# Reordering a two-layer decoder trunk: the order of all work taken from another model, attention's side work dealt by a planner, head halves joined by transfers and POOL

## The chip, the cores and the metric

The kernel runs on one core of a Trainium2 chip. That core has five engines that run at the same time, each with a queue of its own that it works off strictly in order: TensorE (PE; its weight loads are shown apart as PEld), VectorE (DVE), ScalarE (ACT), GpSimd (POOL), and SyncE (SP), which here only issues DMA transfers. The metric is the time of one execution on the device in microseconds; a profile is one such execution, recorded.

## The reference

The program computes a decoder trunk of two layers for 512 tokens of width 1024, in fp32:

```python
h = x
for i in range(2):
    if i == 0:   # RetNet heads and mLSTM heads, chunkwise, one output projection
        h = h + ab_mixer(rms_norm(h, ab_norm_g), ...)
    else:        # sparse attention: 16 query heads, 2 key groups
        h = h + nsa_mixer(rms_norm(h, nsa_norm_g), ...)
    h = h + conv_ffn(rms_norm(h, ffn_norm_g[i]), ...)       # gated, D_FF 2816
    e = rms_norm(p[i] @ ple_w[i], ple_norm_g[i])            # per-layer embedding
    h = h + sigmoid(rms_norm(h, ple_gate_norm_g[i]) @ ple_w_gate[i]) * e

# inside nsa_mixer, for each head and block of 128 queries
o = g[..., 0:1] * o_cmp + g[..., 1:2] * o_slc + g[..., 2:3] * o_win
```

Of the three branches of attention, o_cmp attends to 31 compressed blocks of keys, o_slc to selected blocks, o_win to a window. With 512 tokens the selection takes all blocks and the window reaches all earlier tokens, so o_slc and o_win are two causal softmax attentions over different keys and values.

## The kernel before, in words

Activations stand transposed in SBUF: tiles of 128 features by 512 tokens. Each fp32 matrix product is three matmuls (`mm3`, L148 to L150): both operands are split in a high part, copied to fp32r by ScalarE (`split`, L129), and a low part, the difference, made by VectorE or POOL (L130); high by high, high by low, low by high add up in one PSUM bank. Weights come by 512 KB transfers on SP into a pool of three and are split in the same way (`load`); `lo_seq` says which engine makes the low part. PSUM is dealt as four banks "a", three "b", one "o".

Attention (`nsa_mixer`) goes in steps. Each of the 16 heads has six units, a unit being a block j of 128 queries with one branch or both (96 units in all). A step does the scores of one unit: two matmuls and one that adds the mask (L933 to L935) into an "a" bank, the negative maximum on VectorE (L936), the exponential on ScalarE (L938). When both branches of a block are done, VectorE takes the reciprocal of the sums (L948) and POOL multiplies the probabilities by it and by the gate (L950). Four steps later (`LAG`) TensorE transposes the probabilities into a "b" bank (L961), and ScalarE and VectorE split them into `pt` tiles (L129, L130). Two steps after that the values matmuls (L983) add up in the "o" bank, with two for the compressed branch (L971, L972). A head's output stands in that bank as two halves of 64 rows that have to be added: ScalarE copies one half (L987), VectorE adds the other (L991); every second head, ScalarE and POOL split the pair into `y` tiles for the output projection.

Other work is placed between these steps by step numbers written out by hand (`START`): the products of the per-layer embedding, the query norm of the second eight heads (sums of squares, factor L842 to L848, multiplication on POOL L854, high part on ScalarE L859, low part on VectorE L860), the transpositions of queries (L867), the compressed branch's scores (L887 to L906, eight heads at a time), and the output projection of the first eight heads. The program order is only where the framework starts: its scheduler fixes, before anything is compiled, the order in each engine's queue, by a model of what is ready when and by priorities (`high_priority`, `behind`).

## Time and profile before

| | |
|---|---|
| median of 3 runs | 1390.86 us (1386.83 to 1391.09) |
| profiled execution | 1388.07 us, span 1385.9 us |
| TensorE busy | 1362.8 us, 98% of the span |
| VectorE, ScalarE, POOL busy | 848.2 (61%), 641.3 (46%), 361.3 us (26%) |
| mean granted clock of TensorE | 0.997 |

The span reaches from the first to the last instruction; the execution's own time holds a little more. A busy share is an average over stages with different limits: the mixer of the first layer up to about 200 us, its MLP and embedding gate to about 640, the second layer's projections and compressed keys to 757, attention from 757 to 954, then the output projection, MLP and gate of the second layer. Rows of the trace give a matmul from its issue to its last result, so rows of one engine overlap. A name before `<-` is what an instruction writes, those behind it what it reads; buffer numbers are left out in the trace and stand in the order as `ps_6885`.

### The profile page before, as it was taken

The page shows a single profiled execution, that of the slowest core. Times are in us where ns is not written, and L with a number is a line of the kernel's source. Part 1 is how long each engine was busy: PE and PEld are TensorE (multiplying, and loading weights), DVE is VectorE, ACT ScalarE, POOL GpSimd, SP SyncE. Part 2 cuts the span into 40 slices and gives each one's busy share as a digit, 9 for nine tenths or more (in the row PEclk, how much of TensorE's full clock was granted, in tenths as well). Part 3 has the DMA queues.
Part 4 walks back from the last instruction along what each step waited for, and adds up shares of the span by engine and source line. Part 5 has one row for each costly group of instructions (what it writes and reads, how often), then busy time and mean ns, then how long its engine had stood idle before and what let it go on. Part 6 is the DMA issues. An engine that isn't in the chain of part 4 may idle for free.

```text
span 1385.9 us, 17930 instructions
## 1 busy us (share of the span) xinstructions
PE 1362.8 (98%) x6702; PEld 1119.7 (81%) x6702; DVE 848.2 (61%) x1354; ACT 641.3 (46%) x1125; POOL 361.3 (26%) x360
## 2 busy tenths in 40 slices
PE   9999999999999999999999899999999999999998
PEld 7878788888888888887878677777888888888887
DVE  6765756566356435567858988676565446534555
ACT  5357426444124323455455787676444223313441
POOL 4356502132031101121111755544122022101120
PEclk9999999999999999999999999999999999999999
DMA  6432233232322332233343100111233223333232
GB/s 217 148 104 93 90 98 111 81 106 92 106 83 100 102 96 88 86 119 118 93 138 120 46 2 32 31 32 31 92 97 101 92 79 119 92 96 99 80 107 76
DMA packets 40031, 127.96 MB, mean 92 GB/s; under 512 B 4740, under 2 KB 5380, under 8 KB 39944
## 3 DMA queue, kind: packets, MB, share of 16 engines
q1 hardware_dynamic: 39656, 126.68, 28.8%
q8 instruction: 53, 0.87, 0.2%
q14 instruction: 34, 0.28, 0.1%
q10 hardware_dynamic: 288, 0.14, 0.0%
HBM read 122.60 MB, written 3.15 MB: 91 GB/s over the span
## 4 chain that ended last, share of the span: by engine, by line
PE 85%; DVE 5%; issue 4%; ACT 3%; POOL 3%; DMA 1%; POOLq 0%; ACTq 0%; DVEq 0%
PE ps L148 26%; PE ps L149 25%; PE ps L150 25%; PE ps L961 2%; PE ps L983 2%; ACT pr L938 1%; PE ps L933 1%; PE ps L934 1%; DVE nmx L936 1%; DVE pt L130 1%; POOL y L130 1%; POOL pr L950 1%; ACT wh L129 1%; POOL acc L196 1%; DVE wl L130 1%
## 5 line engine op out<-in xcount | busy, mean ns | idle before, releaser
L148 PE MATMUL ps<-y,wh 128*128 128x512 f32 (+1 forms) x1112 | 434.3, 391 | 1.5 <-ACT y L206 0.6
L149 PE MATMUL ps<-y,wh 128*128 128x512 f32 (+1 forms) x1112 | 431.5, 388 | 0.6 <-POOL y L130 0.6
L150 PE MATMUL ps<-y,wl 128*128 128x512 f32 (+1 forms) x1112 | 431.0, 388 | 0.0
L129 ACT ACTIVATE wh<-wr 128x1024 fp32r<-128x1024 f32 (+2 forms) x223 | 230.2, 1036 | 411.3 <-PE ps L149 344.8
L130 DVE TENSOR_TENSOR wl<-wr,wh 128x1024 fp32r<-128x1024 f32 (+2 forms) x202 | 247.6, 1228 | 46.3 <-ACT wh L129 45.8
L148 PEld LDWEIGHTS ps<-y,wh 128*128 128x128 f32 x1112 | 208.9, 188 | 45.0 <-ACT wh L129 1.0
L150 PEld LDWEIGHTS ps<-y,wl 128*128 128x128 f32 x1112 | 208.8, 188 | 43.6 <-DVE wl L130 0.2
L149 PEld LDWEIGHTS ps<-y,wh 128*128 128x128 f32 x1112 | 208.9, 188 | 43.0 <-POOL y L130 1.1
L1136 POOL TENSOR_TENSOR sc<-sc,rb 128x512 f32<-128x512 f32 x44 | 56.9, 1293 | 476.2 <-ACT sc L1135 476.2
L148 PE MATMUL ps<-gh,wh 128*128 128x512 f32 x352 | 136.9, 389 | 0.0
L149 PE MATMUL ps<-gl,wh 128*128 128x512 f32 x352 | 136.9, 389 | 0.0
L150 PE MATMUL ps<-gh,wl 128*128 128x512 f32 x352 | 136.9, 389 | 0.0
L196 POOL TENSOR_TENSOR acc<-acc,sc 128x512 f32<-128x512 f32 x48 | 74.5, 1553 | 223.6 <-ACT sc L194 223.0
L1151 DVE TENSOR_TENSOR hp<-hp,ps 128x512 f32<-128x512 f32 x48 | 33.0, 688 | 130.3 <-PE ps L150 130.3
L950 POOL TENSOR_SCALAR pr<-pr,sm,gate 128x512 f32<-128x512 f32 (+3 forms) x128 | 78.3, 622 | 74.3 <-DVE sm L948 53.0
L1137 DVE TENSOR_TENSOR sc<-ps,sc 128x512 f32<-128x512 f32 x44 | 30.4, 692 | 92.2 <-POOL sc L1136 85.2
L1129 DVE TENSOR_TENSOR a<-ps,rb 128x512 f32<-128x512 f32 x44 | 30.4, 690 | 92.3 <-PE ps L150 89.5
L150 PEld LDWEIGHTS ps<-gh,wl 128*128 128x128 f32 x352 | 66.1, 188 | 13.8
L148 PEld LDWEIGHTS ps<-gh,wh 128*128 128x128 f32 x352 | 66.1, 188 | 13.7
L149 PEld LDWEIGHTS ps<-gl,wh 128*128 128x128 f32 x352 | 66.1, 188 | 13.6
L1135 ACT ACTIVATE sc<-sc 128x512 f32<-128x512 f32 x44 | 27.8, 632 | 100.8 <-DVE sc L1134 100.8
L938 ACT ACTIVATE pr<-ps,nmx 128x512 f32<-128x512 f32 (+3 forms) x128 | 67.0, 528 | 13.7 <-DVE nmx L936 7.8
(288 smaller groups left out, 2000.8 us busy)
## 6 DMA issues: line engine op xcount, KB each, us to landing
wr<-in_w_up_dram SPq DMA_DIRECT2D x88, 512.0 KB, 3.6
wr<-in_w_down_dram SPq DMA_DIRECT2D x32, 512.0 KB, 3.5
wr<-in_w_plg_dram SPq DMA_DIRECT2D x16, 512.0 KB, 3.6
wr<-in_w_down_dram SPq DMA_DIRECT2D x16, 384.0 KB, 3.0
hp<-in_xT_dram SPq DMA_DIRECT2D x16, 256.0 KB, 4.0
wr<-in_w_abo_dram SPq DMA_DIRECT2D x8, 512.0 KB, 3.6
wr<-in_w_dram SPq DMA_DIRECT2D x8, 512.0 KB, 3.6
wr<-in_w_q_dram SPq DMA_DIRECT2D x8, 512.0 KB, 4.0
```

The lines of the kernel that those rows point to most:

```text
L129: self.nc.scalar.activation(hi, src, AF.Copy)
L130: (eng or self.nc.vector).tensor_tensor(lo, src, hi.bitcast(F32), ALU.subtract)
L148: mm(out, ah, bh, start=first, stop=False)
L149: mm(out, ah, bl, start=False, stop=False)
L150: mm(out, al, bh, start=False, stop=last)
L196: eng.tensor_tensor(n.acc, n.acc, sq, ALU.add)
L938: nc.scalar.activation(pr[:, b], s[:, b], AF.Exp, bias=nmx[:, b : b + 1], accum_out=sm[:, bs[b] : bs[b] + 1])
L950: nc.gpsimd.tensor_scalar(prs[b], prs[b], sm[:, b : b + 1], gate[:, j, hd, 1 + b : 2 + b], ALU.mult, ALU.mult)
L1129: nc.vector.tensor_tensor(a, pa, n.b, ALU.mult)
L1136: nc.gpsimd.tensor_tensor(c, c, n.b, ALU.mult)
L1137: nc.vector.tensor_tensor(c, pb, c, ALU.mult)
L1151: nc.vector.tensor_tensor(self.h[m], self.h[m], ps, ALU.add)
```

## The change

- The scheduler orders all engines' queues by its timeline model (one argument of `TileContext`).
- The units of a head come in the order of blocks 3, 3, 2, 2, 1, 0 instead of 3, 3, 1, 2, 2, 0, and the values of a pair of blocks are issued as the branches of a unit come due. For the blocks 0 and 1 one ScalarE and one VectorE instruction split both branches.
- In place of the step numbers a planner in the kernel deals the side work: for every step it keeps what TensorE, VectorE, ScalarE and POOL (T, V, S, G) have to do in ns, and puts a job at the first step where the backlog over `PACE` per step stays within `SLACK`.
- The compressed branch goes in four groups of four heads.
- A head's whole 128 x 512 output is copied by ScalarE; three transfers per pair of heads on SP bring the halves to the rows where they are added; POOL adds, casts and subtracts. The last pair is joined on VectorE and ScalarE.
- Seven weights in attention get their low part from POOL (`load_late`), four before. The query norm's eight low parts of the second half go from VectorE to POOL, and so do the eight additions of positions to the second kind of blocks (`blocks(1)`).
- The embedding of the second layer is written to DRAM (eight times 256 KB) and read back at the start of the MLP, and its buffers are free meanwhile.
- In the first mixer two projections and the norm's cast change order and banks.

```diff
@@ constants
-UNITS = ((3, (0,)), (3, (1,)), (1, (0, 1)), (2, (0,)), (2, (1,)), (0, (0, 1)))
-START = {"embed": (1, 1), "q_sums": (4, 2), "q_norm": (11, 4), "q_stack": (20, 6), "cmp_scores": 42, ...
+LAG, VALUES_LAG, OUT_WAIT = 4, 2, 3
+PACE, SLACK = 1800, {"T": 2500, "V": 1000, "S": 1000, "G": 1500}
+UNITS = ((3, (0,)), (3, (1,)), (2, (0,)), (2, (1,)), (1, (0, 1)), (0, (0, 1)))
@@ ab_mixer
+            self.cycle = ("o", "b")
+            pm = {0: self.ws(I["w_mqk"][0], n)}
+            self.norm_cast(n)
+            pm[2] = self.ws(I["w_mqk"][2], n)
             self.cycle = ("b", "o")
-            pm = {i: self.ws(I["w_mqk"][i], n) for i in (0, 2)}
-            self.norm_cast(n)
@@ blocks
-                            nc.vector.tensor_tensor(xf[...], view[...], pos, ALU.add)
+                            (nc.gpsimd if which else nc.vector).tensor_tensor(xf[...], view[...], pos, ALU.add)
@@ scale
-                    with self.behind(nc.vector):
-                        nc.vector.reciprocal(sm, sm)
+                    nc.vector.reciprocal(sm, sm)
@@ heads joined: before, in values
-                lo = self.sc()
-                nc.scalar.activation(lo[0:64], po[64:128], AF.Copy)
-                if q % 2 == 0:
-                    self.dst = self.sc()
-                r0 = 64 * (q % 2)
-                nc.vector.tensor_tensor(self.dst[r0 : r0 + 64], po[0:64], lo[0:64], ALU.add)
-                if q % 2:
-                    hi, lo = self.y(), self.y()
-                    self.split(hi, lo, self.dst, nc.gpsimd)
@@ and now, in out_copy and out_parts
+                whole = self.sc()
+                nc.scalar.activation(whole, pos[hd], AF.Copy)
+                if hd % 2 == 0:
+                    part[0], part[1] = whole, self.sc()
+                    nc.sync.dma_start(part[1][0:64], whole[64:128])
+                else:
+                    nc.sync.dma_start(part[0][64:128], whole[0:64])
+                    nc.sync.dma_start(part[1][64:128], whole[64:128])
...
+                return [
+                    lambda: nc.gpsimd.tensor_tensor(one, one, two, ALU.add),
+                    lambda: nc.gpsimd.tensor_copy(hi, one),
+                    lambda: nc.gpsimd.tensor_tensor(lo, one, hi.bitcast(F32), ALU.subtract),
+                ]
@@ planner
+            def fits(e, step, n):
+                late = 0
+                for k in range(step + 12):
+                    late = max(0, late + load[e][k] + n * (k == step) - PACE)
+                    if k >= step and late > SLACK[e]:
+                        return False
+                return True
+
+            def then(step, *jobs):
+                for e, n, f in jobs:
+                    if f is None:
+                        step += n
+                        continue
+                    while not fits(e, step, n):
+                        step += 1
+                    load[e][step] += n
+                    todo[step].append(f)
+                    step += 1
+                return step
...
+                        if hd % 2 and hd < 15:
+                            todo[step + OUT_WAIT].append(lambda step=step, hd=hd: then(step + OUT_WAIT + 1, *zip("GGG", (1290, 620, 1290), out_parts(hd))))
@@ ffn and Embed
             first = mm_up(0)
+            e.back()
...
+            if self.away is not None:
+                self.k.nc.sync.dma_start(self.away[m * P : (m + 1) * P], e)
@@ the program
-    with tile.TileContext(nc) as tc:
+    with tile.TileContext(nc, schedule_with_timeline_sim=True) as tc:
```

How this moves instructions is shown at three places. The first is POOL's queue before, early in attention, where the query norm of the second half (L854) and two weights' low parts (`wl`) stand between scalings of probabilities (L950, `pr`):

```order
L854 TENSOR_TENSOR ep_6151<-ep_6151,tiny_6427 128x512 x2
L854 TENSOR_TENSOR ep_6154<-ep_6154,tiny_6427 128x512
L950 TENSOR_SCALAR pr_6400<-pr_6400,sm_6399,gate 128x256 x2
L854 TENSOR_TENSOR ep_6154<-ep_6154,tiny_6427 128x512
L130 TENSOR_TENSOR wl_8019<-wr_8017,wh_8018 128x1024
L950 TENSOR_SCALAR pr_6443<-pr_6443,sm_6442,gate 128x384
L950 TENSOR_SCALAR pr_6461<-pr_6461,sm_6442,gate 128x384
L130 TENSOR_TENSOR wl_8165<-wr_8163,wh_8164 128x1024
```

And POOL's queue now, at the first join of a pair of heads (addition L1067, cast L1068, subtraction L1069; L997 is the scaling, L900 the query norm's low part):

```order
L997 TENSOR_SCALAR pr_6634<-pr_6634,sm_6633,gate 128x512
L997 TENSOR_SCALAR pr_6657<-pr_6657,sm_6633,gate 128x512
L1067 TENSOR_TENSOR sc_6448<-sc_6448,sc_6450 128x512
L997 TENSOR_SCALAR pr_6677<-pr_6677,sm_6676,gate 128x384
L997 TENSOR_SCALAR pr_6706<-pr_6706,sm_6676,gate 128x384
L997 TENSOR_SCALAR pr_6742<-pr_6742,sm_6741,gate 128x256 x2
L1068 CAST y_6699<-sc_6448 128x512
L997 TENSOR_SCALAR pr_6781<-pr_6781,sm_6780,gate 128x128 x2
L1069 TENSOR_TENSOR y_6700<-sc_6448,y_6699 128x512
L900 TENSOR_TENSOR y_6843<-ep_6098,y_6843 128x4x64
L900 TENSOR_TENSOR y_6844<-ep_6098,y_6844 128x4x64
```

Between the scalings stand the pieces of a join here, one at a time, and behind the last piece all eight query lows (six more follow these two) ahead of the next scaling. Four scalings further on, two weights' low parts follow each other.

The second place is TensorE's queue before, where the scores of attention begin: transpositions of queries (L867), then compressed scores (L887) of 64 columns, 32 in all, around the first scores (L933):

```order
L867 MATMUL ps_6092<-ident,y_5810 128x128
L867 MATMUL ps_6092<-ident,y_5817 128x128
L867 MATMUL ps_6092<-ident,y_5824 128x128
L887 MATMUL ps_6101<-kc,y_5998 128x64
L887 MATMUL ps_6101<-kc,y_6005 128x64
L887 MATMUL ps_6101<-kc,y_6012 128x64
```

The same place now; L161 to L163 are the three matmuls of a product, L930 the compressed scores, L981 and L982 the scores:

```order
L163 MATMUL ps_6051<-w_5129,y_5956 128x64
L930 MATMUL ps_6074<-kc,y_5998 128x64
L930 MATMUL ps_6074<-kc,y_6005 128x64
L981 MATMUL ps_6123<-hp_5119,y_5998 128x512
L982 MATMUL ps_6123<-hp_5121,y_5998 128x512
L930 MATMUL ps_6074<-kc,y_6012 128x64
L930 MATMUL ps_6083<-kc,y_5998 128x64
```

Sixteen compressed scores stand here now instead of 32, with two wide matmuls of the first unit among them, and the transpositions that stood ahead of them are spread elsewhere.

The third place is TensorE's queue in the middle of attention, before: transpositions (L961) of three units follow each other with three or four matmuls between:

```order
L961 MATMUL ps_6885<-ident,pr_6749 128x128 x2
L933 MATMUL ps_6896<-hp_5119,y_6076 128x512
L934 MATMUL ps_6896<-hp_5121,y_6076 128x512
L935 LDWEIGHTS identb
L935 MATMUL ps_6896<-maskb,identb 128x128
L961 MATMUL ps_6902<-ident,pr_6782 128x128 x3
L933 MATMUL ps_6911<-hp_5119,y_6076 128x512
```

And now, with values matmuls (L1037) between two units' transpositions (L1012):

```order
L1012 MATMUL ps_7424<-ident,pr_7337 128x128 x4
L981 MATMUL ps_7528<-ep_5120,y_7160 128x384
L982 MATMUL ps_7528<-ep_5122,y_7160 128x384
L983 LDWEIGHTS identb
L983 MATMUL ps_7528<-maskb,identb 128x128
L1037 MATMUL ps_7386<-pt_7366,vv_5123 64x256
L1037 MATMUL ps_7386<-pt_7365,vv_5123 128x256
L1037 MATMUL ps_7386<-pt_7366,vv_5124 64x128
L1037 MATMUL ps_7386<-pt_7365,vv_5124 128x128
L1037 MATMUL ps_7386<-pt_7366,vv_5123 64x256
L1037 MATMUL ps_7386<-pt_7365,vv_5123 128x256
L1012 MATMUL ps_7448<-ident,pr_7356 128x128 x4
```

Six values matmuls stand between the two units' transpositions in this piece; in the one before there were only scores and masks.

## Rows read from the trace of the kernel before

**Rows 1.** Stretches: length; busy us of PE, PEld, DVE, ACT, POOL; clock; DMA.

```profile
50.00:200.00 150.00, 147.17 (x754) 121.16 (x753) 101.05 (x157) 78.34 (x129) 66.95 (x52) 0.99 0.32 105
200.00:600.00 400.00, 400.00 (x1785) 331.33 (x1784) 213.25 (x268) 151.25 (x192) 65.43 (x47) 1.00 0.31 96
640.00:757.00 117.00, 115.10 (x587) 93.63 (x586) 85.42 (x170) 63.02 (x108) 21.87 (x25) 1.00 0.38 121
757.00:775.00 18.00, 16.26 (x84) 12.69 (x84) 16.03 (x35) 11.28 (x30) 11.39 (x12) 0.91 0.04 7
775.00:800.00 25.00, 20.46 (x143) 16.45 (x143) 22.80 (x54) 21.18 (x61) 19.06 (x21) 1.00 0.18 60
800.00:954.00 154.00, 149.48 (x1051) 120.63 (x1051) 121.69 (x288) 119.87 (x355) 79.66 (x121) 1.00 0.07 22
...
751.45:758.60 7.15, 7.10 (x62) 6.72 (x60) 5.86 (x13) 4.37 (x7) 0.63 (x1) 1.00 0.23 74
758.67:762.08 3.41, 3.41 (x12) 2.50 (x12) 3.04 (x7) 1.71 (x5) 2.33 (x3) 0.50 0.02 5
```

**Rows 2.** Waits, 757 to 955: engine, line, releaser; us in total, times, longest.

```profile
POOL pr L950 <- DVE sm L948: 53.0, 38, 5.1
...
PEld ps L961 <- POOL pr L950: 9.5, 12, 3.1
...
PE ps L961 <- POOL pr L950: 6.8, 9, 3.0
...
PEld ps L961 <- DVE pt L130: 3.3, 9, 0.7
...
PE ps L961 <- DVE pt L130: 1.3, 4, 0.6
```

**Rows 3.** Timeline of PE: start, us, line, operation, tiles, [idle before, releaser].

```profile
785.83 0.82 PE L983 MATMUL ps<-pt,vv 128*64 128x256 f32 x6
786.49 0.40 PE L933 MATMUL ps<-hp,y 128*128 128x512 f32 x1
786.72 0.40 PE L934 MATMUL ps<-hp,y 128*128 128x512 f32 x1
...
790.97 0.55 PE L961 MATMUL ps<-ident,pr 128*128 128x128 f32 x3 [3.01 <-POOL pr L950]
...
857.08 0.33 PE L961 MATMUL ps<-ident,pr 128*128 128x128 f32 x1 [0.30 <-POOL pr L950]
```

**Rows 4.** Timeline of POOL in the same stretch.

```profile
785.89 1.20 POOL L854 TENSOR_TENSOR ep<-ep,tiny 128x512 f32<-128x512 f32 x1
787.06 2.54 POOL L130 TENSOR_TENSOR wl<-wr,wh 128x1024 fp32r<-128x1024 f32 x1
```

**Rows 5.** Groups, 763 to 955: shapes, count, busy us, mean ns; idle before.

```profile
L130 DVE TENSOR_TENSOR pt<-ps,pt 128x512 fp32r<-128x512 f32 x32 | 22.0, 686 | 10.7 <-ACT pt L129 10.6
...
L938 ACT ACTIVATE pr<-ps,nmx 128x512 f32<-128x512 f32 x30 | 20.6, 688 | 4.7 <-DVE nmx L936 3.5 <-DVE sm L948 1.2
L936 DVE TENSOR_REDUCE nmx<-ps 128x1 f32<-128x512 f32 x30 | 20.5, 683 | 0.5
L129 ACT ACTIVATE pt<-ps 128x512 fp32r<-128x512 f32 x32 | 19.2, 600 | 12.1 <-PE ps L961 8.2 <-PE ps L983 3.8
...
L130 POOL TENSOR_TENSOR y<-sc,y 128x512 fp32r<-128x512 f32 x8 | 10.3, 1290 | 5.1 <-ACT y L129 5.1
...
L130 POOL TENSOR_TENSOR wl<-wr,wh 128x1024 fp32r<-128x1024 f32 x4 | 9.7, 2422 | 1.2 <-ACT wh L129 1.2
```

**Rows 6.** Groups of POOL, whole span: the cast.

```profile
L733 POOL CAST st<-st 128x256 fp32r<-128x256 f32 x4 | 1.7, 444 | 4.9 <-DVE st L732 4.9
```

**Rows 7.** One line's instructions on DVE: count, shortest/median/longest ns.

```profile
L860 DVE TENSOR_TENSOR y<-ep,y x16: 412/424/2576, 741.0 to 797.0; 128x256 fp32r<-128x256 f32 x16
```

**Rows 8.** DMA issues: count, KB each, median us to landing.

```profile
sc<-ep SPq DMA_DIRECT2D x16, 64.0 KB, 3.4
...
hp<-keep SPq DMA_DIRECT2D x4, 256.0 KB, 3.5
```

More of the change, by code (lines that the diff above doesn't have):

```diff
@@ L1 @@
+from collections import defaultdict
 from contextlib import ExitStack
@@ L175, in rsqrt, with rsqrt_parts @@
     def rsqrt(self, x, n, p=P):
+        y, root = self.rsqrt_parts(x, n, p)
+        for f in root:
+            f()
+        return y
+    def rsqrt_parts(self, x, n, p=P):
         nc = self.nc
@@ L921, in nsa_mixer, with masked @@
-            parts, unscaled = [], []
+                        for q in range(4):
+                            nc.tensor.matmul(ps[:, jj, q], qs[4 * me.c + q][:, j * P : (j + 1) * P], kc[:, :, g], start=True, stop=True)
+                def masked(me, jp):
+                    js, ps = slice(2 * jp, 2 * jp + 2), me.ps[jp]
+                    e4 = me.e.rearrange("p (j h n) -> p j h n", j=4, h=4)[:, js]
+                    nc.vector.tensor_tensor(e4, ps[:, :, :, 0], maskc[:, js].unsqueeze(2).to_broadcast([P, 2, 4, 32]), ALU.add)
+                    nc.vector.tensor_tensor(e4, e4, ps[:, :, :, 1], ALU.add)
@@ L923, in scores, with low @@
+                def low(me):
+                    nc.vector.tensor_tensor(pcs[me.c][1], me.pt, pcs[me.c][0].bitcast(F32), ALU.subtract)
+            parts, unscaled = {}, []
             def scores(hd, j, bs):
@@ new lines, in stack, with comp_first @@
+            def stack(sts, hd, s0):
+                got = []
+                copy = "VS"[hd % 2 == 0], 620, lambda: q_stack_copy(hd, got[0])
+                last = then(s0, ("T", 440, lambda: got.append(q_stack_t(sts, hd, "b" if s0 < LAG else "a"))), copy)
+                assert last <= 6 * hd, ("stack", hd, last)
+                return last
+            def comp_first(c, s0):
+                got = {}
+                x = lambda name, *a: lambda: getattr(got["x"], name)(*a)
+                last = then(s0, ("T", 530, lambda: (got.update(x=Compressed(c, "a")), got["x"].products(0))))
+                then(last, ("V", 840, x("masked", 0)))
+                last = then(last, ("T", 530, x("products", 1)), ("V", 840, x("masked", 1)))
+                last = comp_last(got, last, ("V", 680, x("maxima")), ("G", 1050, x("shift")), ("", 1, None))
+                assert last <= 24 * c + LAG + VALUES_LAG + 2, (c, last)
@@ new lines, in comp_last, with late @@
+            def comp_last(got, s0, *jobs):
+                x = lambda name: lambda: getattr(got["x"], name)()
+                last = then(s0, *jobs, ("S", 630, x("exp")), ("V", 1100, x("factors")), ("G", 1050, x("scaled")), ("", 2, None), ("T", 440, x("turned")), ("S", 600, x("high")), ("V", 690, x("low")))
+                return last
+            def late(step, src, use):
+                got = []
+                todo[max(step - 8, 0)].append(lambda: got.extend(self.load_late(src)))
+                then(max(step - 6, 2), ("S", 1060, lambda: got[1]()), ("G", 1500, lambda: got[2]()))
+                todo[step].append(lambda: use(got[0]))
@@ new lines, in embed, with out_first @@
+            def embed(m, s0):
+                got = []
+                then(s0, ("T", 1360, lambda: got.append(emb.products(m, ew[m // 4]))), ("S", 600, lambda: emb.keep(m, got[0])))
+            def out_first(m, s0):
+                got = []
+                then(s0, ("T", 2720, lambda: got.append(self.out_products(wo[m // 2], m, *outs[0]))), ("V", 690, lambda: self.out_add(m, got[0])))
+            wo = {}
+            for step, e, n, f in ((0, "S", 630, comp.exp), (1, "V", 1100, comp.factors), (2, "G", 1050, comp.scaled), (4, "T", 440, comp.turned), (5, "S", 600, comp.high), (6, "V", 690, comp.low)):
+                load[e][step] += n
+                todo[step].append(f)
@@ new lines, in nsa_mixer @@
+            comp_first(1, max(stack(sts, 4 + i, 2 + 2 * i) for i in range(4)) + 1)
+            ss1 = self.small(32)
+            r1, root1 = q_factor(ss1)
+            last = 0
+            for t in range(NTT):
+                a, b = q_sums(zq, ss1, t, nc.gpsimd)
+                last = max(last, then(3 + t, ("G", 1050, a), ("V", 690, b)))
+            for k in (0, 4, 7):
+                last = then(last, ("V", 600, lambda k=k: [f() for f in root1[k : k + (4 if k == 0 else 3)]]))
+            for t in range(NTT):
+                a, b, c = q_norm(zq, r1, t, sts1, nc.gpsimd)
+                ready_at = then(last + t, ("G", 1050, a), ("S", 800, b), ("G", 1300, c))
@@ new lines, in nsa_mixer @@
+            todo[51].append(lambda: self.fetch(self.keep, (0, 2)))
+            live, ready, done = {}, defaultdict(list), []
+            for step in range(len(seq) + 40):
+                lows, sums = [], done[:]
+                done.clear()
+                for hd in sums:
+                    out_copy(hd)
+                if 0 <= step - LAG < len(seq):
+                    hd, j, bs = seq[step - LAG]
+                    lows = probs(hd, j, bs, live.pop(step - LAG))
+                    if j % 2 == 0:
+                        ready[step + VALUES_LAG].append((hd, j // 2, bs))
```

346 lines of the change are left out of this document (189 added, 157 removed).

## The prediction

> **What bounds the kernel now.** I read the stretch table first [rows 1]: busy time of each engine by stretch, with TensorE's granted clock. TensorE is busy for 400.00 of the 400.00 us between 200 and 600, with 1785 matmuls, so one 512-column matmul starts every 0.224 us and none waits. That stretch is the gated MLP of the first layer; the second layer's runs the same code. The change can give nothing there, and can lose only if a weight arrives late. What can be won lies where TensorE is less than full: 2.83 us idle in 50 to 200 (mixer of the first layer), 1.90 in 640 to 757 (second layer ahead of attention), and in attention 1.74 in 757 to 775, 4.54 in 775 to 800 and 4.52 in 800 to 954, together 10.80. No other engine is full: in 800 to 954 VectorE has 121.69 of 154 us, ScalarE 119.87, POOL 79.66. So the kernel is bound by TensorE's stream, broken in attention by short waits.
>
> Idle time understates a break. A matmul's row lasts 0.40 us while the next starts 0.23 later (the first two PE rows of [rows 3]), so a break of the stream by x shows as x − 0.17 idle. The waits of PE and of its weight loads in attention come to some 34 that name a releaser [rows 2]; with about ten that don't, I take 45 breaks and 45 × 0.17 = 7.6 us more. Attention loses 10.8 + 7.6 = 18.4 us, by this estimate.
>
> Who ends them [rows 2]: transpositions (L961) wait for POOL's scaling of the probabilities (L950), 6.8 us in 9 waits, longest 3.0, and 1.3 for VectorE's low parts, which free the PSUM bank the transpositions write. POOL itself waits 53.0 us in that stretch, nearly all for VectorE's reciprocal: it is late, not short of time. The 3.01 us wait shows how [rows 3, 4]: POOL does one multiplication of the query norm (L854, 1.20) and the low part of a weight (2.54) ahead of the 384-wide scaling that TensorE stands for. Order, then, not amount.
>
> **The change part by part.** The matmuls are the same in number and shape, so TensorE's own work is the same; the sum is over breaks. It is made against the profiled execution, 1388.07 us (span 1385.9).
>
> 1. *Distance from scores to transpositions.* I counted the matmuls between the end of a unit's scores and its first transposition, each by the distance at which its shape follows itself in the trace (0.227 us for 512 columns, about 0.11 for a 128-wide transposition or a 256-column values matmul, whose six rows take 0.82 us in [rows 3]). Before: least 3.6 us, middle 6.7. After: least 6.1, middle 8.9. Short waits recur in the trace at the units with 4.4 (0.30 idle at 857.08 [rows 3], with 0.17 a break of 0.47), so the chain of maximum, exponential, reciprocal and scaling needs about 4.9 us; after the change no unit has less than that with nothing else in POOL's queue. Likewise for the three transposition banks: from one tenant's last transposition to the first of the next but two, 23 of 121 had under 1.6 us of matmuls before, none after. ScalarE's high copy and VectorE's low need about 1.3 (0.600 and 0.686 [rows 5]). Of 18.4 us these two hold all but the start and the tail.
>
> 2. *Against it.* (a) Score banks: before, none was refilled within 2.4 us of its last matmul; after, about 20 of 96 are, the nearest in 1.35. A refill needs the maximum and the exponential, 0.683 + 0.688 [rows 5] plus hand-overs, about 2.0. I take 0.1 us for each of 20: 2.0; bounds 0 and 20 × 0.65 = 13. (b) Eight query lows (L900) stand in a row on POOL ahead of a 512-wide scaling. A 256-wide one is not in the trace on POOL; half of the 512-wide subtraction's 1.290 [rows 5] is 0.65, so 5.2 us; four scalings on, two weights' lows follow each other, 2 × 2.422. Against some 3 us of slack (a distance of 8 less 4.9) I take 3.0 lost there, once; bounds 0 and 10. (c) The joins, seven pairs: an addition, a cast, a subtraction. The subtraction was POOL's before (1.290). The cast lies between 0.444 (the row half as wide [rows 6]) and 0.89, taken as 0.65; the addition is new there and is put near the subtraction: 1.29. That adds 7 × (1.29 + 0.65) = 13.6 us to POOL. It takes three more lows of weights as well, 3 × 2.422 = 7.3, and the eight query lows, 5.2. POOL's load in attention goes from some 56% to some 75%: room on average, the risk is in place. A join's addition waits for transfers between partitions, which the nearest row puts at 3.4 us for 64 KB (128 KB here) [rows 8]; two to four scalings are queued in front of it after the copy, about 2 to 3 us. I take a wait of 0.5 us for each of seven, covered by item 1's slack: nothing on TensorE; bounds 0 and 7 × 3.4 = 23.8. (d) VectorE loses 14 of its 16 additions and the eight query lows, ScalarE's join copies go from 64 to 128 rows at the same width: nothing on the path, bounds −1 and 0.
>    The start of attention and its last units keep about 1.3 us. So 18.4 − 2.0 − 3.0 − 1.3 = 12.1 gained in attention.
>
> 3. *The clock.* For 3.41 us from 758.67 the granted clock is 0.50, that is 1.2 of 2.4 GHz, after 7.15 us in which TensorE ran 62 matmuls, nearly all narrow, back to back at 1.00 [rows 1]. The stretch holds 12 matmuls where 3.41 / 0.227 = 15 would go, so it costs 3.41 / 2 = 1.7 us at most. After the change that narrow run is cut by two 512-column matmuls and is shorter by 16 transpositions and 16 products. I take 1.6 gained; bounds 0 and 1.7.
>
> 4. *First mixer.* 2.83 us idle, about 2 more hidden in 12 breaks, and a second such half-clock stretch (0.99 of 150 us is 1.5). Products of the denominators move later and are spread between wide matmuls. I take 2.4 of these 6.3; bounds −2 and 6.
>
> 5. *Ahead of attention.* 1.90 us idle, about 2.5 with what is hidden. Additions for the second half of the blocks move to POOL, which has 21.87 of 117 us there. I take 0.5; bounds −2 and 2.5.
>
> 6. *Embedding kept in DRAM.* Eight writes and eight reads of 256 KB on SP; reads landed in 3.5 us [rows 8], are issued with the first MLP product and are wanted many microseconds later. Nothing, and 3.5 us if a weight is held up behind them.
>
> Sum: 12.1 + 1.6 + 2.4 + 0.5 = 16.6, so 1371.5 in the terms of the profiled execution. That lies 2.8 below the median shown and inside the runs' spread (1386.83 to 1391.09); I add half of it: **1373 us**.
>
> **One rule weighed.** In attention VectorE's query lows (L860) take up to 2.576 us where the least is 0.412 [rows 7], about as long as POOL's low of a weight (2.422 [rows 5]). The Trainium skill ("SBUF — State Buffer", Who interferes with whom) says why: an instruction of VectorE with two inputs in SBUF and one of POOL that reads SBUF lock each other out for a whole instruction; one with an input in PSUM does not take part. The trace agrees, for the lows of the probabilities, which read PSUM, stay at 0.686. By the rule, more work on POOL stretches none of VectorE's 128 probability lows and the sum stays; were it false, and each stretched by a tenth, VectorE would lose some 6 us of time that it has idle.
>
> **The rivals.** *Only the large breaks go* (0.22). The small waits come back at the score banks: item 2a near the upper third, 10 us. Then 16.6 − 8 = 8.6 gained in the sum: 1381. For it: ScalarE and VectorE are at 78 to 79% in 800 to 954. Against it: the middle refill distance is 3.8 us, nearly twice the need. *POOL becomes the bound, slower* (0.09). Place: the additions L1067, which hold POOL until the transfers have landed, with the scalings behind them. Price 7 × 3.4 = 23.8, and the lows of item 2b at their full 10, 7 more: 1373 + 30.8 = 1404. It decides from about 2.5 us lost on TensorE at each join: from there on nothing is left of the gain. For it: POOL's scaling is what TensorE waits for already. Against it: 6.1 us at least between scores and transpositions. *No change* (0.12). The model that orders the work evens out attention, but refills and the first mixer pay it back (2a at its bound of 13, item 4 at −2): 16.6 − 11 − 4.4 = 1.2, so 1388. *All breaks go* (0.06): 18.4 + 1.7 + 6 + 2.5 = 28.6, some 1361.
>
> **How the numbers follow.** Forecast 0.51, within 1364 to 1379. Range: the forecast and the first rival with it, up to the edge of the third: 1361 to 1389; outside are the slow rival and some of the third. A measurement here tells 0.3% from nothing, 4.2 us: 1386.7 to 1395.0. Faster: 0.51 + 0.06 + 0.22 + a fifth of the third, 0.81. Same 0.11, slower 0.08.
>
> **What would show it.** Right: in attention no wait of a transposition for POOL above 1 us but at item 2b's place; TensorE above 97% in the stretch that holds the middle heads; the granted clock at 1.00 where attention begins. Wrong: waits of scores (L981) for ScalarE's exponential above 5 us in all; POOL standing for a DMA ahead of L1067 with transpositions waiting for the scaling behind it; new idle time of TensorE in either MLP. The forecast fails if attention, from the first scores to the last values, is not some 10 us shorter.

## The result and the profile after

The changed kernel takes 1380.12 us (median of 6 runs, 1377.30 to 1380.46), the kernel before, run alongside, 1390.16: a ratio of 0.9927, 95% interval 0.9912 to 0.9942. Its profiled execution took 1380.31 us, span 1378.6. So it is faster by 10 us, 0.7%, clear of the noise, where the sum had 16.6. Stretches after, columns as in [rows 1]; the stages up to attention start at most 3 us earlier than before, and attention's last values end 4 us earlier:

```profile
50.00:200.00 150.00, 150.00 (x764) 123.22 (x764) 98.60 (x155) 79.25 (x129) 63.92 (x51) 1.00 0.35 105
200.00:600.00 400.00, 400.00 (x1786) 331.59 (x1785) 214.76 (x271) 152.40 (x194) 68.20 (x47) 1.00 0.31 97
640.00:757.00 117.00, 111.82 (x560) 91.47 (x559) 79.60 (x154) 58.64 (x103) 30.52 (x31) 0.99 0.37 116
757.00:775.00 18.00, 13.84 (x73) 9.75 (x71) 17.79 (x42) 13.72 (x33) 14.41 (x16) 1.00 0.23 75
775.00:800.00 25.00, 24.88 (x172) 20.91 (x172) 19.96 (x49) 16.99 (x50) 15.67 (x22) 0.93 0.19 58
800.00:850.00 50.00, 49.22 (x365) 40.42 (x364) 39.07 (x90) 43.10 (x129) 43.36 (x58) 1.00 0.25 75
850.00:948.00 98.00, 97.79 (x686) 82.69 (x685) 68.30 (x151) 68.05 (x196) 61.73 (x85) 1.00 0.15 39
727.80:731.20 3.40, 3.40 (x10) 2.66 (x9) 2.65 (x7) 1.36 (x2) 0.00 (x0) 0.51 0.75 219
775.80:779.20 3.40, 3.40 (x17) 3.19 (x16) 1.92 (x5) 1.05 (x3) 3.40 (x4) 0.52 0.53 181
```

The first mixer has no idle time left (2.83 us before). From 775 on attention has 0.12 + 0.78 + 0.21 idle in place of 9.06. But 757 to 775 has 4.16 where it had 1.74, the stretch ahead of attention 5.18 where it had 1.90, and the granted clock falls to half twice, at 727.8 and 775.8, as it did before at two other places (161.3 and 758.7).

For an account that idle time does not understate, I took, from the distance between each matmul's start and the next one's, the middle distance for the shape of the later one in both kernels. What is left over (below: "by starts"), in us:

| stretch | before | after |
|---|---|---|
| 0 to 200 | 4.5 | 2.1 |
| 640 to 757 | 5.5 | 9.5 |
| 757 to 775 | 3.5 | 5.8 |
| 775 to 955 | 7.9 | −2.6 |
| whole span | 21.5 | 14.3 |

The difference, 7.2, is that of the spans, 7.3. (Below zero: a middle distance holds some waiting itself.) The levels hang on this choice: set against the shape of the earlier matmul, attention from 775 on comes to some 19 before and 9 after. The differences between the two kernels stay within 0.3 us of those in the table, and the argument rests on them.

Waits of TensorE, 757 to 948, that answer to [rows 2]:

```profile
PE ps L981 <- DVE y L913: 2.5, 1, 2.5
PE ps L959 <- POOL sc L954: 0.7, 1, 0.7
...
PE ps L1037 <- DVE pt L1247: 0.2, 1, 0.2
```

No transposition of the probabilities (L1012) waits for POOL's scaling any more (6.8 us before); one of the compressed branch (L959) does, for 0.7. POOL itself now stands for the joins' transfers:

```profile
POOL sc L1067 <- DMA sc<-sc: 14.9, 5, 6.5
POOL pr L997 <- DVE sm L995: 11.4, 10, 2.5
```

The wait that is left at the start of attention, 2.45 us, in the timelines of PE, DVE and POOL:

```profile
775.12 0.45 PE L981 MATMUL ps<-hp,y 128*128 128x384 f32 x1 [2.45 <-DVE y L913]
```

```profile
769.84 0.99 DVE L204 TENSOR_TENSOR tiny<-tiny 128x32 f32<-128x32 f32 x1
...
772.20 1.81 DVE L204 TENSOR_TENSOR tiny<-tiny 128x32 f32<-128x32 f32 x1
...
774.38 0.68 DVE L913 CAST y<-ps 128x512 fp32r<-128x512 f32 x1
```

```profile
769.73 1.04 POOL L954 TENSOR_TENSOR sc<-sc,tiny 128x512 f32<-128x512 f32 x1
...
771.61 2.36 POOL L143 TENSOR_TENSOR wl<-wr,wh 128x1024 fp32r<-128x1024 f32 x1
```

A multiplication of 32 columns (a Newton step of the query norm) lasts 0.99 and 1.81 us on VectorE, and ends each time when POOL's instruction ends (770.77 and 773.97). The copy of queries (L913) that TensorE needs stands behind it in VectorE's queue.

The kernel before had the same thing once, which I overlooked: at 771.25 a Newton step of VectorE (L182) lasted 2.33 us beside a weight's low part on POOL. The trace shows no wait of TensorE for another engine between 757 and 779 there, so it cost nothing that can be seen (DVE, POOL):

```profile
771.25 2.33 DVE L182 TENSOR_TENSOR tiny<-tiny 128x32 f32<-128x32 f32 x1
```

```profile
771.15 2.38 POOL L130 TENSOR_TENSOR wl<-wr,wh 128x1024 fp32r<-128x1024 f32 x1
```

Ahead of attention TensorE waits for low parts of the compression's weights (L803), and between them for a high and a low part of the query projection's (L161, L162):

```profile
690.82 0.33 PE L803 MATMUL ps<-wl,pt 128*64 128x256 f32 x1 [2.14 <-DVE wl L134]
...
723.13 1.20 PE L161 MATMUL ps<-wh,y 128*128 128x512 f32 x4 [0.74 <-ACT wh L133]
725.60 0.33 PE L803 MATMUL ps<-wl,pt 128*64 128x256 f32 x1 [1.28 <-DVE wl L134]
...
727.33 0.50 PE L162 MATMUL ps<-wl,y 128*128 128x512 f32 x1 [0.58 <-DVE wl L134]
```

What stands ahead of these low parts, at 690 (ACT, then DVE) and at 725 (DVE):

```profile
688.46 1.10 ACT L133 ACTIVATE wh<-wr 128x1024 fp32r<-128x1024 f32 x1
```

```profile
689.54 1.22 DVE L134 TENSOR_TENSOR wl<-wr,wh 128x1024 fp32r<-128x1024 f32 x1
...
720.61 2.49 DVE L878 TENSOR_TENSOR sc<-ep 128x512 f32<-128x512 f32 x4
...
723.15 1.26 DVE L880 TENSOR_REDUCE tiny<-sc 128x8 f32<-128x512 f32 x2
724.34 1.21 DVE L134 TENSOR_TENSOR wl<-wr,wh 128x1024 fp32r<-128x1024 f32 x1
```

### The profile page after: what moved, and what is told of

It reads as the page before. It is cut to its first block, busy times and chain, and to the rows that moved or that the text cites. A ratio compares the mean times of both kernels' runs of the same rounds, so it can differ in the third digit from the quotient of the medians.

```text
span 1378.6 us, 17917 instructions
## 1 busy us (share of the span) xinstructions
PE 1361.5 (99%) x6702; PEld 1123.8 (82%) x6702; DVE 832.8 (60%) x1294; ACT 629.2 (46%) x1086; POOL 393.9 (29%) x392
## 4 chain that ended last, share of the span: by engine, by line
PE 91%; DVE 3%; ACT 3%; issue 1%; POOL 1%; DMA 1%; SPq 0%; POOLq 0%; ACTq 0%
PE ps L161 27%; PE ps L163 27%; PE ps L162 26%; PE ps L1037 3%; PE ps L1012 2%; PE ps L981 1%; PE ps L982 1%; PE ps L391 1%; POOL acc L219 1%; DVE wl L134 1%; ACT pr L986 0%; PE ps L256 0%; PE ps L248 0%; PE ps L983 0%; PE ps L459 0%
## 5 line engine op out<-in xcount | busy, mean ns | idle before, releaser
L133 ACT ACTIVATE wh<-wr 128x1024 fp32r<-128x1024 f32 (+2 forms) x216 | 223.3, 1036 | 459.2 <-PE ps L162 366.8
L161 PE MATMUL ps<-y,wh 128*128 128x512 f32 (+1 forms) x1112 | 431.7, 390 | 0.2 <-ACT wh L133 0.2
L162 PE MATMUL ps<-y,wh 128*128 128x512 f32 (+1 forms) x1112 | 430.4, 388 | 0.0
L163 PE MATMUL ps<-y,wl 128*128 128x512 f32 (+1 forms) x1112 | 429.3, 389 | 0.3 <-DVE wl L134 0.3
L163 PEld LDWEIGHTS ps<-y,wl 128*128 128x128 f32 x1112 | 208.7, 188 | 44.0 <-DVE wl L134 0.7
L161 PEld LDWEIGHTS ps<-y,wh 128*128 128x128 f32 x1112 | 208.8, 188 | 43.6 <-ACT wh L133 0.7
L162 PEld LDWEIGHTS ps<-y,wh 128*128 128x128 f32 x1112 | 208.9, 188 | 41.8
L161 PE MATMUL ps<-gh,wh 128*128 128x512 f32 x352 | 136.9, 389 | 0.0
L162 PE MATMUL ps<-gl,wh 128*128 128x512 f32 x352 | 136.6, 389 | 0.0
L163 PE MATMUL ps<-gh,wl 128*128 128x512 f32 x352 | 136.3, 389 | 0.0
L997 POOL TENSOR_SCALAR pr<-pr,sm,gate 128x512 f32<-128x512 f32 (+3 forms) x128 | 76.8, 619 | 16.5 <-DVE sm L995 11.4
L163 PEld LDWEIGHTS ps<-gh,wl 128*128 128x128 f32 x352 | 66.1, 188 | 13.8
L162 PEld LDWEIGHTS ps<-gl,wh 128*128 128x128 f32 x352 | 66.1, 188 | 13.8
L161 PEld LDWEIGHTS ps<-gh,wh 128*128 128x128 f32 x352 | 66.1, 188 | 13.6
L1247 DVE TENSOR_TENSOR pt<-ps,pt 128x512 fp32r<-128x512 f32 (+1 forms) x96 | 56.5, 595 | 19.7 <-ACT pt L1015 19.3
```

The source lines that it names most:

```text
L133: self.nc.scalar.activation(hi, src, AF.Copy)
L161: mm(out, ah, bh, start=first, stop=False)
L162: mm(out, ah, bl, start=False, stop=False)
L163: mm(out, al, bh, start=False, stop=last)
L997: nc.gpsimd.tensor_scalar(prs[b], prs[b], sm[:, b : b + 1], gate[:, j, hd, 1 + b : 2 + b], ALU.mult, ALU.mult)
L1247: nc.vector.tensor_tensor(*lows, ALU.subtract)
```

## The experiments

Each time is the median, each ratio that to the kernel before run alongside, with its 95% interval. The scheduler orders all queues anew for each variant, so a variant can differ from its base by more than its edit.

**model_only** and **planner_only**: each half of the change alone.

```diff
 # model_only: the kernel before        # planner_only: the changed kernel
-    with tile.TileContext(nc) as tc:
+    with tile.TileContext(nc, schedule_with_timeline_sim=True) as tc:    # planner_only: the reverse
```

> The kernel before, with the timeline model ordering the queues and nothing else changed. Theory A (the gain in attention comes from the planner's spacing, the gain in the first mixer and the loss ahead of attention from the model): first mixer 2.5 us shorter, ahead of attention 3 to 4 longer, attention about as before: 1388 to 1392. Theory B (the model makes the whole gain): 1378 to 1382.

> The changed kernel with the default model ordering the queues. Theory A: attention still gains some 8 us, the first mixer and the stretch ahead of attention stay as in the kernel before: 1380 to 1383. Theory B (the planner is worth nothing without the model): 1387 or more, with the waits of transpositions for POOL's scaling back.

Measured: model_only 1412.99 us, 1.0180 (1.0166 to 1.0193); planner_only 1391.72, 1.0029 (1.0017 to 1.0041). Neither half alone is faster. For model_only both theories fail, and it is 21 us above the top of theory A's range. For planner_only theory B's time and its sign come true, the waits of transpositions for POOL's scaling: 14.0 us in all. That the planner is worth nothing without the model does not follow (see default_join_old). Of theory A one thing holds: the first mixer gains with the model alone (70 to 200, by starts: 2.5 us less left over than in planner_only, and the same as in the changed kernel). In model_only attention loses most, and the largest wait has the cause seen above (PE, DVE, POOL):

```profile
789.67 0.90 PE L961 MATMUL ps<-ident,pr 128*128 128x128 f32 x3 [4.86 <-DVE pt L130]
```

```profile
783.02 2.28 DVE L184 SCALAR_TENSOR_TENSOR tiny<-tiny,tiny 128x32 f32<-128x32 f32 x1
...
786.43 2.28 DVE L183 SCALAR_TENSOR_TENSOR tiny<-tiny,tiny 128x32 f32<-128x32 f32 x1
```

```profile
782.90 2.35 POOL L130 TENSOR_TENSOR wl<-wr,wh 128x1024 fp32r<-128x1024 f32 x1
...
786.32 2.34 POOL L130 TENSOR_TENSOR wl<-wr,wh 128x1024 fp32r<-128x1024 f32 x1
```

In planner_only my slow rival is there to be seen: POOL reaches the join's addition before the transfers, and scalings stand behind it (POOL, then PE):

```profile
848.65 1.30 POOL L1067 TENSOR_TENSOR sc<-sc,sc 128x512 f32<-128x512 f32 x1 [2.91 <-DMA sc<-sc]
850.01 0.61 POOL L1068 CAST y<-sc 128x512 fp32r<-128x512 f32 x1
850.58 1.05 POOL L942 TENSOR_TENSOR sc<-sc,tiny 128x512 f32<-128x512 f32 x1
851.59 1.27 POOL L1069 TENSOR_TENSOR y<-sc,y 128x512 fp32r<-128x512 f32 x1
852.84 2.82 POOL L997 TENSOR_SCALAR pr<-pr,sm,gate 128x512 f32<-128x512 f32 x4
```

```profile
853.67 1.12 PE L1012 MATMUL ps<-ident,pr 128*128 128x128 f32 x4 [3.72 <-POOL pr L997]
```

**join_old** and **default_join_old**: heads joined as before, with either order.

```diff
-                nc.scalar.activation(whole, pos[hd], AF.Copy)
-                nc.sync.dma_start(...)        # three per pair
...
+                nc.scalar.activation(whole[0:64], pos[hd][64:128], AF.Copy)
+                nc.vector.tensor_tensor(part[0][r0 : r0 + 64], pos[hd][0:64], whole[0:64], ALU.add)
...
-                    lambda: nc.gpsimd.tensor_tensor(one, one, two, ALU.add),
-                    lambda: nc.gpsimd.tensor_copy(hi, one),
+                    lambda: None,
+                    lambda: nc.scalar.activation(hi, one, AF.Copy),
```

> The changed kernel with the heads joined as before (ScalarE copies 64 rows, VectorE adds, ScalarE makes the high part, POOL the low part), at the planner's steps; 21 transfers, seven additions and seven casts of POOL go. Theory A (with the model's order the joins' transfers cost TensorE nothing, item 2c of the prediction): within 1.5 us of the changed kernel, 1379 to 1382. Rival (VectorE's 14 additions stand in front of the low parts that free the transposition banks): 3 to 6 us longer, 1383 to 1386, with waits of transpositions or values for VectorE.

> The same joins, with the default model ordering the queues; to be compared with planner_only (1391.72 us). Theory D (there POOL stands for the joins' transfers ahead of scalings that TensorE waits for: 14.4 us of waits of the addition for a transfer, and breaks of 3.1, 3.8 and 3.9 us behind them): the breaks behind the additions go, those behind POOL's low parts of weights (one of 3.8 us) stay: 6 to 9 us shorter, 1383 to 1386. Rival (POOL is simply too full): 1 to 3 us shorter, 1389 or more.

Measured: join_old 1380.35, 0.9922 (0.9908 to 0.9935); default_join_old 1385.29, 0.9962 (0.9950 to 0.9975). Theory A and theory D hold. With the model's order the way of joining heads is worth nothing, in either direction; with the default order the transfers and POOL's additions cost 6.4 us (by the medians of planner_only and default_join_old), and the break behind two weights' low parts stays (3.3 us idle ahead of 820.1). So the planner is not worthless without the model: with the old joins it is faster than the kernel before by 0.4%, clear of the noise, and transpositions wait 6.7 us for POOL's scaling where planner_only has 14.0. With these joins the model's order brings another 4.9 us (join_old).

**hidden_pool**: the low parts of the compression's weights on POOL.

```diff
+                    self.lo_seq = "g"
                     hi, lo = self.load(I["w1"][which, c])
+                    self.lo_seq = "v"
```

> The changed kernel with the low parts of the eight compression weights made by POOL. Theory A (TensorE's 2.1 us and 0.7 to 1.5 us waits at 688 and 722 to 727 come from VectorE's queue, where those low parts stand behind other work): the waits go and with them the half-clock stretch behind them, 4 to 5 us shorter, 1375 to 1376. Rival (the weights themselves arrive late, or POOL's 2.4 us for each is the new wait): 1380 to 1383, with waits of the same products for POOL or for ScalarE's high parts.

Measured: 1380.28, 0.9946 (0.9933 to 0.9958). The rival holds. TensorE's waits at 687 to 692 became longer (PE, POOL):

```profile
687.97 0.33 PE L805 MATMUL ps<-wl,pt 128*64 128x256 f32 x1 [1.05 <-POOL wl L134]
...
692.00 0.47 PE L805 MATMUL ps<-wl,pt 128*64 128x256 f32 x1 [2.88 <-DVE gate L731]
```

```profile
685.56 2.36 POOL L134 TENSOR_TENSOR wl<-wr,wh 128x1024 fp32r<-128x1024 f32 x1 [2.85 <-ACT wh L133]
687.89 1.75 POOL L748 TENSOR_TENSOR sc<-sc 128x256 f32<-128x256 f32 x3
689.61 2.34 POOL L134 TENSOR_TENSOR wl<-wr,wh 128x1024 fp32r<-128x1024 f32 x1
```

The second is put down to VectorE's gate, but POOL's low part ended at 691.95, just ahead of the matmul. Behind it the granted clock was 0.5 for 6.8 us from 690.8, where the changed kernel's profile has 3.4 us at 727.9. TensorE uses a weight up in 0.93 us here (8 matmuls) and three follow each other; VectorE needs 1.2 for a low part, POOL 2.4.

**spread**: the same products, two weights, then one after each of the next two steps of the query projection. The edit is shown for the first product; the second is done alike, and the transpositions of both results (`hidden_t`) move behind the third step.

```diff
-            hk = hidden(0, xk)
+            hidden(ph, 0, xk, (0, 1))
             q0 = self.Tokens(self, I["w_q"][0], n)
-            q0.steps(0, 2)
+            q0.steps(0, 1)
+            hidden(ph, 0, xk, (2,))
+            q0.steps(1, 2)
+            hidden(ph, 0, xk, (3,))
...
```

> The changed kernel with the eight weights of the compression products spread: two, then one after each of the two next steps of the query projection, in place of four in a row. Theory E (three weights used within 2.8 us are more than ScalarE and VectorE can split and the transfers bring in that time, whoever makes the low parts): the waits of 2.1 us at 688 and 0.7 to 1.5 at 722 to 727 go, and the half-clock stretch behind them: 5 us shorter, 1374 to 1376. Rival (the order on VectorE there is at fault): waits of the same size at other products, 1379 to 1381.

Measured: 1376.95, 0.9906 (0.9893 to 0.9920), 3.2 us below the changed kernel; the intervals still overlap. Theory E holds in part: the wait at 690 for a weight of the compression is gone, and the stretch ahead of attention has 3.58 idle at full clock,

```profile
640.00:757.00 117.00, 113.42 (x574) 92.63 (x573) 81.70 (x159) 62.75 (x111) 34.31 (x35) 1.00 0.40 124
757.00:775.00 18.00, 12.96 (x75) 10.02 (x74) 17.10 (x41) 10.53 (x29) 14.24 (x16) 0.91 0.19 65
```

5.8 left over by starts in place of 9.5; of the 3.7 gained at most 1.7 is the half-clock stretch that is gone. But the rival is there too: a wait of 1.4 us for VectorE stands at another product,

```profile
690.33 0.50 PE L162 MATMUL ps<-wl,y 128*128 128x512 f32 x1 [1.43 <-DVE wl L134]
```

and two for ScalarE, of 0.9 and 0.8. So how much was the weights' pace and how much the order on VectorE and ScalarE stays open. And 1.3 of the gain comes back in the first 18 us of attention, where TensorE now waits 4.0 us for POOL in the compressed branch.

**newton_pool** and **model_newton**: the second half's Newton steps on POOL, in the changed kernel and in model_only. The lines show what runs there in place of what; the other square roots keep the old lines.

```diff
-            nc.vector.tensor_tensor(t, y, y, ALU.mult)
-            nc.vector.scalar_tensor_tensor(t, t, -0.5, x, ALU.mult, ALU.mult)
-            nc.vector.scalar_tensor_tensor(y, t, 1.5, y, ALU.add, ALU.mult)
+            g.tensor_tensor(t, y, y, ALU.mult)        # g = nc.gpsimd
+            g.tensor_tensor(t, t, x, ALU.mult)
+            g.tensor_scalar(t, t, -0.5, 1.5, ALU.mult, ALU.add)
+            g.tensor_tensor(y, y, t, ALU.mult)
```

> The changed kernel with the three Newton steps of the query norm's second half on POOL. Theory C (VectorE's 32-column multiplications at 768 to 774 last 0.50, 0.99 and 1.81 us because an instruction of POOL holds SBUF's shared port; behind them stands the copy of queries that TensorE waits 2.45 us for): the wait at 772 goes, the half-clock stretch behind it too, 2.5 to 4 us shorter, 1376 to 1378. Rival (VectorE's queue is simply too full there, or the wait moves to POOL's scalings behind the new steps): 1379 to 1382.

> model_only (1412.99 us) with the three Newton steps of the second half on POOL; the weights' low parts stay on POOL, one just ahead of the steps. Theory C (in model_only two of VectorE's 32-column steps last 2.28 us each beside POOL's low parts of weights at 782.9 and 786.3, and TensorE waits 5.0 us for the low part behind them): no 32-column step of VectorE above 1 us is left in attention's first 40 us, the wait of 5.0 us goes or is under 1.5: 4 to 8 us shorter, 1405 to 1409. Rival (the wait is the order's, whoever makes the steps; now the steps stand behind the weights on POOL): the wait moves to what needs the query norm, 1411 to 1415.

Measured: newton_pool 1376.14, 0.9907 (0.9892 to 0.9923); model_newton 1408.94, 1.0140 (1.0119 to 1.0161), 4.0 below model_only. Theory C holds both times: the 2.45 us wait and the 4.86 us wait are gone, and both times lie in its ranges. Against model_only the gain is clear of the noise; newton_pool's interval overlaps the changed kernel's, so there it rests on the trace. In newton_pool the clock stays at 1.00 from 757 on:

```profile
757.00:775.00 18.00, 15.97 (x92) 11.83 (x91) 15.90 (x35) 12.67 (x31) 15.44 (x18) 1.00 0.22 74
775.00:800.00 25.00, 25.00 (x189) 21.18 (x188) 20.56 (x50) 21.08 (x62) 22.49 (x38) 1.00 0.24 69
```

**late_pieces**: POOL's low parts in four instructions.

```diff
-lambda: self.nc.gpsimd.tensor_tensor(lo, raw, hi.bitcast(F32), ALU.subtract)
+lambda: [self.nc.gpsimd.tensor_tensor(lo[:, s : s + 256], raw[:, s : s + 256], ...) for s in range(0, 1024, 256)]
```

> The changed kernel with POOL's low parts of the seven weights in attention made in four instructions of 256 columns in place of one of 1024; VectorE's work is as it was. Theory C (an instruction of POOL shuts out VectorE's instructions with two inputs in SBUF until it ends): the longest of VectorE's 32-column Newton steps at 768 to 774 falls from 1.81 us to under 1.1, TensorE's wait of 2.45 us for the copy of queries behind them to 0.5 to 1.7: 1 to 2 us shorter, 1378 to 1379.5. Rival (VectorE's queue is too full there): the wait stays, and POOL, a little slower, adds to it: 1380 to 1382.

Measured: 1379.57, 0.9933 (0.9919 to 0.9946), so no difference in time that can be told. In the trace the steps beside the four pieces last about one piece each (DVE), the longest of the nine is 0.99 us, and TensorE's wait falls from 2.45 to 1.75 (PE), just above theory C's 1.7. This run separates the causes best: VectorE has the same work as in the changed kernel, and only the length of POOL's instruction differs.

```profile
771.25 0.64 DVE L204 TENSOR_TENSOR tiny<-tiny 128x32 f32<-128x32 f32 x1
...
772.61 0.65 DVE L206 SCALAR_TENSOR_TENSOR tiny<-tiny,tiny 128x32 f32<-128x32 f32 x1
```

```profile
774.13 0.44 PE L981 MATMUL ps<-hp,y 128*128 128x384 f32 x1 [1.75 <-DVE y L913]
```

How long a step is held follows POOL's instruction; with shorter ones more steps are held.

**lows_dve**: the second half's query lows and multiplications on VectorE.

```diff
-                a, b, c = q_norm(zq, r1, t, sts1, nc.gpsimd)
+                a, b, c = q_norm(zq, r1, t, sts1, nc.vector)
```

> The changed kernel with the query norm's eight low parts of the second half, and its four multiplications, on VectorE as far as the planner had them on POOL (the planner's table unchanged). Theory C: VectorE's subtractions have two inputs in SBUF; several of them last 1 us and more where alone they take 0.42, and TensorE waits for what stands behind them: 1381 to 1384. Rival (item 2b of the prediction: the row of eight on POOL costs TensorE 3 us): 1376 to 1378.

Measured: 1381.36, 0.9944 (0.9930 to 0.9959); against the changed kernel within the noise, with two new waits of TensorE, 1.2 us idle ahead of 810.4 and 0.9 ahead of 814.4. The rival fails: the row on POOL cost no 3 us. Of theory C only a part is seen: not several of the lows but one is held, for 1.839 us (least, middle, longest):

```profile
L900 DVE TENSOR_TENSOR y<-ep,y x16: 394/407/1839, 738.2 to 812.7; 128x256 fp32r<-128x256 f32 x16
```

**spread_newton** and **no_tiny_pairs**: the two gains together, and one more small product moved to POOL.

```diff
-                    nc.vector.tensor_tensor(sm3, sm3, gate[:, :, 4 * me.c : 4 * me.c + 4, 0], ALU.mult)
+                    nc.gpsimd.tensor_tensor(sm3, sm3, gate[:, :, 4 * me.c : 4 * me.c + 4, 0], ALU.mult)
```

> Both: the weights spread and the three Newton steps of the second half on POOL (alone 1376.14 us, 4.0 us shorter). Theory E with C: the gains add up, 1370 to 1373. Rival: 1375 to 1377, the gain of the Newton steps alone.

> spread_newton with one more instruction moved from VectorE to POOL, the 128x16 product of the reciprocal sums with the gates in the compressed branch (four of them). In spread_newton it lasted 2.12 us beside POOL's low part of a weight (765.50 to 767.84), and TensorE waited 4.0 us for what comes after it. Theory C: that wait goes, or is under 1.5 us: 3 to 4 us shorter than spread_newton (1376.24), 1372 to 1373.5. Rival (the chain is late whatever engine has it): 1375.5 to 1377.

Measured: spread_newton 1376.24, 0.9902 (0.9888 to 0.9915); no_tiny_pairs 1376.84, 0.9915 (0.9902 to 0.9929). The rivals hold: the gains do not add up. TensorE now comes to the compressed branch before that branch's own chain is done. In spread_newton one small product of the chain is held up beside a low part of a weight, and the scaling behind it ends at 769.1 (DVE, POOL, PE):

```profile
765.76 2.12 DVE L959 TENSOR_TENSOR tiny<-tiny,gate 128x16 f32<-128x16 f32 x1
```

```profile
765.50 2.34 POOL L143 TENSOR_TENSOR wl<-wr,wh 128x1024 fp32r<-128x1024 f32 x1
768.02 1.05 POOL L962 TENSOR_TENSOR sc<-sc,tiny 128x512 f32<-128x512 f32 x1 [0.18 <-DVE tiny L201]
```

```profile
769.12 0.66 PE L967 MATMUL ps<-ident,sc 128*128 128x128 f32 x4 [4.01 <-POOL sc L962]
```

In no_tiny_pairs that product takes 0.22 us on POOL, but the scaling L962 then stands behind the same low part in POOL's own queue (766.32 to 768.66), ends at 770.0, and TensorE waits 4.32 us. Whether the low part behind that scaling would help was not run. newton_pool, spread, spread_newton and no_tiny_pairs, 1376.1 to 1377.0 us, beat both kernels by their medians; only spread_newton's interval lies nearly clear of the changed kernel's.

## Why the prediction was right, and where its size was off

The direction, the place and the mechanism of item 1 were right: what the change takes away is transpositions waiting for POOL's scaling and for VectorE's low parts, 8.1 us of idle time in [rows 2], none after (one values matmul waits 0.2 for a low part). That planner, order and joins hang together I did not say: planner_only has 14.0 us of such waits for POOL, 6.7 when the joins are the old ones, and model_only waits for VectorE and ScalarE instead.

That the time lies in the stated range is in part luck. 1380.12 is outside the forecast's own 1364 to 1379 and next to the 1381 of the first rival, which widened the range; but that rival's cause, 10 us of waits at the score banks, did not come. Between the profiled executions, which are 7.8 us apart, the gain is 10.5 in attention from 775 on and 2.4 in the first mixer, less 4.0 lost ahead of attention and 2.3 at its start, where I had put next to nothing. Of the signs that I named, the transpositions' waits and TensorE's share in the middle heads (97.79 of 98 us) came; the clock fell once more, at 775.7. The last sign did not: from the first scores to the last values attention takes 193.3 us where it took 194.4, not 10 less. It was badly chosen, since the first scores now start 2.9 us earlier and 47 more matmuls lie between the two ends (1306 for 1259), by the middle distances some 6 us of work.

*Item 2.* (a) Score banks: the waits for the exponential show 0.4 us idle at each of three places, together 1.6 by starts; I took 2.0. (b) The row of eight lows starts at 808.6, ends at 814.2 and cost TensorE nothing; I took 3.0. A 256-wide low took 0.737 us on POOL (0.65 estimated), the cast 0.627 (0.65), the addition 1.295 (1.29). (c) POOL waits 14.9 us for transfers, more than the 3.5 I allowed, and TensorE does not see it; join_old confirms the zero for the model's order, and with the default order it is 6.4 us. The transfers of 128 KB land in 2.3 us, sooner than the 3.4 of [rows 8].

*The pool of breaks* I put at 18.4 us in attention, of it 7.6 by 45 breaks that hide 0.17 each. Its true size the trace does not settle: by starts it is 11.4 with the shape of the later matmul and some 23 with that of the earlier. Gained there, with the clock, by either: 8.2, where items 1 to 3 together had 13.7. The term that was mis-sized for certain is the 1.3 left for attention's start and tail: 757 to 775 alone has 4.16 us idle, more than half of it the wait behind the Newton steps.

*The step that failed is item 5.* I took 0.5 gained ahead of attention, with −2 as the worst; it lost 4.0, at most 1.7 of it by the half-clock stretch at 727.9. I weighed POOL's load there and not the order on VectorE and ScalarE: the compression's weights are used up (0.93 us each) faster than any one engine splits them (1.2 and 2.4). At 690 the low part begins as ScalarE's high part ends (689.56). At 725 the model's order has put four squares and two sums of the query norm (720.61 to 724.41) ahead of the low part that TensorE stands for from 724.3. model_only has the same three waits (0.9, 1.4, 0.7 by starts), planner_only 0.36 and 0.33, so they come with the model's order. The wait of 2.1 us at 690 is longer than in either.

*Item 3 failed too*: the half-clock stretch at 758.7 went, that at 161 went with the first mixer's breaks, and two others came, each behind a stretch with waits: behind 722 to 727 and behind the 2.45 us wait at 772. Where those waits are taken away (newton_pool at 775) or made less (spread at 727), the clock stays at 1.00 there, but spread has a half-clock stretch at 769.1 instead, beside its 4.0 us wait.

*The rule that I weighed* was the right one, and I drew too little from it. An instruction of VectorE with two inputs in SBUF and one of POOL that reads SBUF shut each other out (the Trainium skill, "SBUF — State Buffer", Who interferes with whom). The trace agrees: a low of the probabilities, with one input in PSUM, lasts 0.68 us while POOL scales (L1247 at 768.88), and 32-column Newton steps of 0.2 us last until POOL's instruction ends, with whatever stands behind them in VectorE's queue. [rows 7] showed 2.576 us already, and the Newton step at 771.25 of the kernel before 2.33. It is not that more low parts stand on POOL there: between 757 and 800 three begin in the kernel before (771.15, 787.06, 791.69) and one in the changed one (771.61). The order has changed, so that a copy TensorE needs now stands close behind the held steps. I asked which long instructions of VectorE are touched, not what stands behind the short ones.

*Items 4 and 6* held: 2.4 gained in the first mixer (2.4 taken, of a pool of 6.3, so the match is close by chance; at most 1.7 of it is the half-clock stretch at 161), nothing for the embedding's way over DRAM.

## What to carry to other kernels

Cost an instruction on POOL also by what it locks: list VectorE's instructions with two SBUF inputs that may run beside it, however small, and what is queued behind them. Whether the scheduler's model counts this lock no run shows; so read each gain and each loss by stretch, not by the sum: here 13 us gained in two stretches (2.4 and 10.5 by starts) and 6 lost in two others (4.0 and 2.3). A wait that is taken away in a stretch with a chain of its own (the compressed branch) comes back at that chain's end; check where the next chain ends before adding up gains. And try the parts of a change in pairs: one that costs nothing under one order (the joins) cost 6.4 us under the other, and hid what the planner gains alone.

## What the runs showed of the hardware

Beside instructions of POOL of 2.34 to 2.38 us, instructions of VectorE of 16 and 32 columns with two inputs in SBUF lasted 2.12 to 2.33 us (model_only, spread_newton, the kernel before); one with a single input, a 32-column scalar operation in no_tiny_pairs, lasted 2.30 as well (766.40, L201). The Trainium skill ("SBUF — State Buffer", Who interferes with whom) says that `tensor_scalar`, under conditions on its operands, can enter a two-port mode and then contends with GpSimd, and the trace agrees in this one case. How often a half-clock stretch comes, and behind which waits, was only seen, not tested: newton_pool and lows_dve have the same 2.1 us wait at 690 as the changed kernel, and in their profiled executions the clock fell to half there, in the changed kernel's it did not. The runs of the changed kernel are 1377.3 and 1377.8 us at a mean clock of 0.998 to 0.999, and 1380.0 to 1380.5 at 0.995 to 0.997.
